# Gated DeltaNet stage of a two-layer decoder: a triangular solve merged to 128 ahead of the recurrence, squares and tanh written to PSUM banks, output norm once per group

## The chip, the cores and the metric

One core of a Trainium2 chip runs the whole program. The metric is the device time of one execution in microseconds (us). Engines are named as in the profile: PE (matmul; PEld its weight loads), DVE (VectorE), ACT (ScalarE), POOL (GpSimd) and SP (which here issues the DMAs). PSUM is the memory that PE writes its results to, in eight banks of 128 x 512 floats; the rest of the tiles lie in SBUF.

## The reference

A residual stream of 16 meta tokens and 256 tokens (272 x 2048, fp32) goes through two layers. The first mixes the tokens by a gated DeltaNet, the second by differential attention; each is followed by a squared-ReLU MLP of width 8192. The change lies in the first mixer:

```python
def gated_deltanet(h, w_in, conv_w, a_log, dt_bias, o_norm, w_out):
    proj = h @ w_in                        # 2048 -> q, k (16 heads), v, z (32 heads), beta and decay logits
    qkv = silu(causal_depthwise_conv(qkv, conv_w))         # 4 taps
    q, k = l2_normalize(q) * 128 ** -0.5, l2_normalize(k)
    beta, g = sigmoid(b_logit), -exp(a_log) * softplus(a_logit + dt_bias)
    o = chunk_gated_delta_rule(q, k, v, beta, g)
    o = rms_norm(o, o_norm) * silu(z)
    return o @ w_out

def step(S, (qc, kc, vc, bc, gc)):         # one chunk of tokens, S the state of a head
    G = cumsum(gc); decay = exp(G_i - G_j) for j <= i
    a_kk = strict_lower(bc * kc @ kc.T * decay)
    sol = triangular_solve(I + a_kk, [vc * bc, kc * bc * exp(G)])
    v_new = u - w @ S
    o = (qc * exp(G)) @ S + (qc @ kc.T * decay) @ v_new
    S = S * exp(g_last) + (kc * exp(g_last - G)).T @ v_new
```

## The kernel before

Activations lie with the features on the partitions. Each weight is read as 128 x 1024 floats twice per tile, and split: ACT copies it to a rounded `whi` (L137), DVE or POOL subtracts to get `wlo` (L141). A product is then three matmuls per 128 x 128 block, `whi*xh`, `wlo*xh` and `whi*xl` (L154, L157, L158), over 272 columns, in one PSUM bank out of a ring of four (`psm`).

The DeltaNet (`gdn`) goes over eight groups of four value heads and two key heads. A group takes 4 projections for its keys and queries (`keys`), 4 for its values (`values`) and 4 for its gates (`gates`). `conv_silu` runs the 4 taps (ACT L615, DVE L618), then tanh (ACT L620) and `out = (tanh + 1) * ac` on DVE (L621). `gate_out` multiplies the output of the group two places back by its slice of `w_out` and adds into `acc` (DVE L982).

The tokens of a group are cut in chunks of 128, 128 and 16. `products` makes for each chunk `ua`: in its first half the scaled, masked product of the keys (the triangle to solve, transposed and negated), in its second that of keys and queries. The 16 x 16 blocks on the diagonal go to DRAM, `solve` inverts all of them at once on DVE by rows (`forward`, L629 and L630), and they come back as `DT`, block-diagonal. POOL clears the blocks of `ua` on and below the 16-diagonal (`below`, L733).

`core` is the recurrence of the group. Its sub-generator `merge(c)` makes, from the 16-blocks, the inverses of the 32-blocks (`ps_e`, `ps_d`), has POOL clear `ua` below the 32-diagonal too, and multiplies them with it (`ps_n`, copied to `NT`). Then each of the chunks 0 and 1 takes the right-hand side `R`, applies `NT` three times in turn (`ps_a` L885, copies and adds L892, L896, L899), which sums the series over the four 32-blocks, and multiplies by the 32-block inverses: `ps_w` (L905), copied to `w`; DVE scales it to `ws` (L913). `ps_s` (from `ws`) gives the next state, `ps_o` (from `w`) the output. Chunk 2 needs no series. Each chunk ends in its output norm: four squares with row sums (ACT L942), eleven small DVE instructions (L944 to L948 with the seven of `rsqrt`, L105 to L111), one scaling (DVE L949); `turned` then transposes it (`ps_ot` L809) and multiplies it into the gates (L811).

The order of the instructions comes from `Flow`, a heap of generators: while projections are written, each k-step advances a clock by its nominal time, and a generator whose time has come writes its next piece between them. A generator that yields `step` (3.0, in the last group 2.0) asks to be called that much later. So the recurrence of group b-1 lies in small pieces between the projections of group b; after them the engines take their queues strictly in that order. In the last group there are only the products of `gate_out(6)` to lie between. `gate_out(7)` then ends the mixer: behind each of its 16 tiles DVE adds into `acc`, and `squares` adds up the squares of `acc` for the RMS norm (`add_ss`: ACT L183, for the last two tiles DVE L185; DVE adds into `ss` at L190). `token_means` sums `ss` over the partitions on PE (`pst`, L213), and the MLP waits for that.

## Time and profile before

| what | value |
|---|---|
| time, median of 3 runs | 3111.37 us (3111.28 to 3116.6) |
| time of the profiled execution | 3111.88 us |
| its span, first to last instruction | 3110.1 us |
| PE busy / PEld busy | 3010.9 us (97%) / 2946.4 us (95%) |
| DVE / ACT / POOL busy | 1930.1 us (62%) / 1443.3 us (46%) / 660.7 us (21%) |
| mean granted TensorE clock | 0.987 |
| the DeltaNet stage | from the start to about 1136 us |

The page gives for each engine the time in which it was busy, the span in 40 slices, and groups of instructions by line. "Idle before, releaser" is the time in which an engine stood still ahead of such an instruction, and what ended it. The view by windows gives busy times in chosen stretches of the span, with the mean clock that PE was granted. Times in us, unless marked ns. fp32 matmuls show as two records each (two passes); the split ones as one.

### The profile page before, as it was taken

To read this page: it belongs to the slowest core of one execution; us is meant where nothing else is said; L and a number is where in the kernel's file an instruction comes from. 1 tells how busy PE (TensorE), PEld (TensorE's weight loads), DVE (VectorE), ACT (ScalarE), POOL (GpSimd) and SP (SyncE) were. 2 spreads that over 40 slices of the span, in tenths; PEclk is the share of its full clock that TensorE was granted. 3 is DMA by queue.
4 is the path that set the end of the run, shared out by engine and by line. 5 is a ranking of instruction groups with operands and counts; after the bars stand their busy time and mean duration, and the time that the engine had idled before them with its cause. 6 is when DMAs were issued, how large, how long until landed. Compare 5 with 4: busy or idle time off the path is not lost. (4 is left out here: it accounts for less than half of the span.)

```text
span 3110.1 us, 57337 instructions
## 1 busy us (share of the span) xinstructions
PE 3010.9 (97%) x23779; PEld 2946.4 (95%) x23779; DVE 1930.1 (62%) x3449; ACT 1443.3 (46%) x2565; POOL 660.7 (21%) x398
## 2 busy tenths in 40 slices
PE   7999999999998889999999999999999999999998
PEld 6988999999998889999999999999999999999998
DVE  7676574766748485455555557777756555555555
ACT  4445454454544345434444334555555444444443
POOL 2544445545454351000000003400004000000000
PEclk9999999999999989999999999999999999999999
DMA  4433334334343335454444443443354555555553
GB/s 178 151 117 122 133 118 151 133 125 158 117 152 103 119 145 183 176 176 172 171 174 175 176 176 123 177 149 136 138 189 163 189 186 183 188 189 180 188 190 109
DMA packets 92468, 488.36 MB, mean 157 GB/s; under 512 B 29104, under 2 KB 32528, under 8 KB 34736
## 3 DMA queue, kind: packets, MB, share of 16 engines
q1 hardware_dynamic: 92208, 484.70, 43.7%
q8 instruction: 187, 3.06, 0.4%
q14 instruction: 73, 0.60, 0.1%
HBM read 481.41 MB, written 3.25 MB: 156 GB/s over the span
## 5 line engine op out<-in xcount | busy, mean ns | idle before, releaser
L137 ACT ACTIVATE whi<-wraw 128x1024 fp32r<-128x1024 f32 x890 | 939.2, 1058 | 1180.3 <-PE ps_dn L158 435.9
L141 DVE TENSOR_TENSOR wlo<-wraw,whi 128x1024 fp32r<-128x1024 f32 x682 | 841.4, 1237 | 717.1 <-ACT whi L137 715.9
L141 POOL TENSOR_TENSOR wlo<-wraw,whi 128x1024 fp32r<-128x1024 f32 x208 | 503.7, 2424 | 1584.3 <-ACT whi L137 1572.5
L158 PE MATMUL ps_dn<-yl,whi 128*128 128x272 f32 (+1 forms) x2048 | 584.5, 285 | 0.0
L157 PE MATMUL ps_dn<-yh,wlo 128*128 128x272 f32 (+1 forms) x2048 | 583.2, 285 | 0.0
L154 PE MATMUL ps_dn<-yh,whi 128*128 128x272 f32 (+1 forms) x2048 | 583.2, 285 | 0.0
L154 PE MATMUL ps_up<-xh,whi 128*128 128x272 f32 (+1 forms) x2048 | 582.9, 285 | 0.0
L158 PE MATMUL ps_up<-xl,whi 128*128 128x272 f32 (+1 forms) x2048 | 582.0, 285 | 0.1
L157 PE MATMUL ps_up<-xh,wlo 128*128 128x272 f32 (+1 forms) x2048 | 581.5, 285 | 0.2 <-DVE wlo L141 0.2
L154 PE MATMUL ps_in<-xh,whi 128*128 128x272 f32 x1520 | 463.4, 305 | 0.0
L157 PE MATMUL ps_in<-xh,wlo 128*128 128x272 f32 x1520 | 442.4, 291 | 16.7 <-DVE wlo L141 13.3
L158 PE MATMUL ps_in<-xl,whi 128*128 128x272 f32 x1520 | 444.0, 292 | 3.3 <-DVE xl L319 3.3
L154 PEld LDWEIGHTS ps_up<-xh,whi 128*128 128x128 f32 x2048 | 386.2, 189 | 0.5 <-ACT xh L402 0.2
L158 PEld LDWEIGHTS ps_dn<-yl,whi 128*128 128x128 f32 x2048 | 386.6, 189 | 0.0
L154 PEld LDWEIGHTS ps_dn<-yh,whi 128*128 128x128 f32 x2048 | 386.3, 189 | 0.0
L158 PEld LDWEIGHTS ps_up<-xl,whi 128*128 128x128 f32 x2048 | 385.6, 189 | 0.3 <-DVE xl L410 0.3
L157 PEld LDWEIGHTS ps_dn<-yh,wlo 128*128 128x128 f32 x2048 | 385.2, 188 | 0.0
L157 PEld LDWEIGHTS ps_up<-xh,wlo 128*128 128x128 f32 x2048 | 384.7, 188 | 0.5 <-DVE wlo L141 0.5
L157 PEld LDWEIGHTS ps_in<-xh,wlo 128*128 128x128 f32 x1520 | 290.2, 191 | 20.3 <-DVE wlo L141 14.9
L154 PEld LDWEIGHTS ps_in<-xh,whi 128*128 128x128 f32 x1520 | 289.7, 191 | 7.8 <-issue 5.1
L158 PEld LDWEIGHTS ps_in<-xl,whi 128*128 128x128 f32 x1520 | 289.5, 190 | 4.8 <-DVE xl L319 3.7
L399 POOL TENSOR_TENSOR hT<-hT,t_res 128x272 f32<-128x272 f32 (+1 forms) x40 | 34.9, 894 | 742.9 <-DVE t_res L391 698.2
(305 smaller groups left out, 4833.8 us busy)
## 6 DMA issues: line engine op xcount, KB each, us to landing
wraw<-w_up SPq DMA_DIRECT2D x128, 1024.0 KB
wraw<-w_down SPq DMA_DIRECT2D x128, 1024.0 KB
wraw<-w_in SPq DMA_DIRECT2D x97, 1024.0 KB
wraw<-w_out SPq DMA_DIRECT2D x32, 1024.0 KB
wraw<-w_kv SPq DMA_DIRECT2D x32, 1024.0 KB
wraw<-w_q SPq DMA_DIRECT2D x16, 1024.0 KB
wraw<-w_o SPq DMA_DIRECT2D x16, 1024.0 KB
gb<-g_dram SPq DMA_DIRECT2D x8, 544.0 KB
```

Source lines behind the costliest of these rows:

```text
L137: nc.scalar.activation(hi, part, AF.Copy)
L141: inst = eng.tensor_tensor(lo, part, hi.bitcast(F32), ALU.subtract)
L154: one = nc.tensor.matmul(ps, wh, rh, start=(k == 0), stop=False)
L157: nc.tensor.matmul(ps, wl, rh, start=False, stop=False)
L158: ring["mm"] = nc.tensor.matmul(ps, wh, rl, start=False, stop=(k == nk - 1))
L399: put(key, eng.tensor_tensor(h, h, ts[m][:, :N], ALU.add))
```

## The change

- **Solve.** `merge` now goes on from the 32-blocks to the 64-blocks and the whole 128-block, so that `dt` is the full inverse; the three applications of `NT` are gone, and `ps_w` multiplies `dt` with `R` at once. Each of three levels is a pair of products, of which only the blocks that change are made (64, 32 and 64 columns wide), with ACT copies between them, into the constant tiles `AE1`, `AE2`, `AE3`, `dt` and `dn`. Both calls of `below` are gone, as the products read only the blocks of `ua` that they need.
- **Banks.** `conv_silu` writes tanh over the projection's own PSUM bank; in the last `gate_out` the squares, but for the first and the last, go to the bank just added into `acc`; the output norm's squares go over `ps_o`.
- **Scaling by beta** (`ws`) is four ACT instructions from `ps_w`, ahead of the copy to `w`.
- **Output norm** once per group (12 columns) and for the last group still per chunk; the scaling is by ACT, four instructions per chunk. Each chunk's `turned` is added after that, 2.0 apart.
- One buffer fewer in the ring of work tiles (`G1`); `r0` shares the buffer of `ss`.

```diff
--- before.py
+++ after.py
-G1 = 8
+G1 = 7
...
+TGAP = 2.0
...
-    def add_ss(ss, src, m, N, eng):
+    def add_ss(ss, src, m, N, eng, bank=None):
 
         if m == 0:
             ss.append(npool.tile([P, L], F32, tag="ss", name="ss", bufs=1))
             return [nc.scalar.activation(ss[0][:, :N], src, AF.Square)]
-        sq = npool.tile([P, L], F32, tag="sq", name="sq", bufs=SQ)
-        if m < KT - NSQ or eng is nc.gpsimd:
+        if bank is None or m == KT - 1:
+            sq = npool.tile([P, L], F32, tag="sq", name="sq", bufs=SQ)
+        else:
+            sq = bank
+        if m < KT - NSQ or eng is nc.gpsimd or bank is not None:
             one = nc.scalar.activation(sq[:, :N], src, AF.Square)
         else:
             one = nc.vector.tensor_tensor(sq[:, :N], src, src, ALU.mult)
...
-    r0 = npool.tile([P, L], F32, name="r0", bufs=1)
+    r0 = npool.tile([P, L], F32, tag="ss", name="r0", bufs=1)
...
+    AE1 = gc.tile([P, HB, P], F32, name="AE1")
+    AE2 = gc.tile([P, HB, 64], F32, name="AE2")
+    AE3 = gc.tile([P, HB, 64], F32, name="AE3")
+    nc.gpsimd.tensor_copy(AE1, ident[:, None, :].broadcast_to([P, HB, P]))
+    nc.gpsimd.memset(AE2, 0.0)
+    nc.gpsimd.memset(AE3, 0.0)
 
     def conv_silu(ps, m, out):
 
         ac = gt.tile([P, L], F32, tag="g272", name="cv_a", bufs=GB)
-        th = gt.tile([P, L], F32, tag="g272", name="cv_x", bufs=GB)
         x = ps
         if m in unscaled:
-            x = th
+            x = gt.tile([P, L], F32, tag="g272", name="cv_x", bufs=GB)
             nc.vector.tensor_tensor(x, ps[:, :L], r0, ALU.mult)
         nc.scalar.activation(ac, x[:, :L], AF.Copy, scale=gdnc[:, m, 3:4])
         for j in (2, 1, 0):
             sh = 3 - j
             nc.vector.scalar_tensor_tensor(ac[:, sh:], x[:, :L - sh], gdnc[:, m, j:j + 1], ac[:, sh:],
                                            ALU.mult, ALU.add)
+        th = ps[:, :L]
         nc.scalar.activation(th, ac, AF.Tanh, scale=0.5)
         nc.vector.scalar_tensor_tensor(out, th, 1.0, ac, ALU.add, ALU.mult)
 
                 for bl in range(8):
                     q = slice(NM * bl, NM * bl + NM)
                     nc.sync.dma_start(scr[c, :, bl].rearrange("h j i -> j h i"), ua[q, :, 0, q])
-                below(ua, NM)
             else:
...
         step = STEP7[0] if b == NB - 1 else STEP
+        outs = []
+        ms = gt.tile([P, len(CH), HB], F32, tag="o_ms", name="o_ms")
+        nc.vector.memset(ms, 1.0)
         merged = {}
 
         def flat(t):
@@ -822,35 +828,68 @@
 
         def merge(c):
 
+            U = UA[c][:, :, 0, :]
+            X = DT[:, c].rearrange("p h (b i) -> p (h b) i", i=32)
             us = work("us")
             nc.gpsimd.affine_select(us.rearrange("p h (b i) -> p h b i", i=32),
-                                    UA[c][:, :, 0, :].rearrange("p h (b i) -> p h b i", i=32),
+                                    U.rearrange("p h (b i) -> p h b i", i=32),
                                     pattern=[[0, HB], [-32, 4], [0, 32]], base=0, channel_multiplier=1,
                                     compare_op=ALU.is_ge, fill=0.0)
-            below(UA[c], 32)
-            e16 = work("e16")
-            nc.vector.transpose(flat(e16), flat(DT[:, c]))
+            en = work("e16")
+            nc.vector.transpose(flat(en), flat(DT[:, c]))
             yield step
-            _, pE = bank("ps_e")
+
+            def small(name):
+                t = psc.tile([P, 512], F32, tag="c", name=name)
+                return t, t[:, 0:256].rearrange("p (h i) -> p h i", h=HB)
+
+            _, pE = small("ps_e")
+            ev = en.rearrange("p h (b i) -> p h b i", i=32)
             for hv in range(HB):
-                nc.tensor.matmul(pE[:, hv], us[:, hv], e16[:, hv], start=True, stop=True)
-            ae = work("ae")
-            nc.scalar.copy(ae, pE)
+                nc.tensor.matmul(pE[:, hv], us[:, hv], ev[:, hv, :, 0:NM], start=True, stop=True)
+            nc.scalar.copy(AE1.rearrange("p h (b i) -> p (h b) i", i=32)[:, :, 0:NM],
+                           pE.rearrange("p h (b i) -> p (h b) i", i=NM))
+            dt = work("d32")
+            dv = dt.rearrange("p h (b i) -> p (h b) i", i=32)
+            nc.scalar.copy(dv[:, :, 0:NM], X[:, :, 0:NM])
             yield step
-            _, pD = bank("ps_d")
+            _, pD = small("ps_d")
             for hv in range(HB):
-                nc.tensor.matmul(pD[:, hv], ae[:, hv], DT[:, c, hv], start=True, stop=True)
-            d32 = work("d32")
-            nc.vector.tensor_tensor(d32, DT[:, c], pD, ALU.add)
+                nc.tensor.matmul(pD[:, hv], AE1[:, hv], X[:, 4 * hv:4 * hv + 4, NM:32], start=True, stop=True)
+            nc.scalar.copy(dv[:, :, NM:32], pD.rearrange("p h (b i) -> p (h b) i", i=NM))
             dn = work("dn")
-            nc.vector.transpose(flat(dn), flat(d32))
+            nc.vector.transpose(flat(dn), flat(dt))
             yield step
-            _, pN = bank("ps_n")
+            pairs = lambda t, hv, k: t[:, hv].rearrange("p (b k i) -> p b k i", k=2, i=32)[:, :, k]
+            _, pE = small("ps_e")
             for hv in range(HB):
-                nc.tensor.matmul(pN[:, hv], dn[:, hv], UA[c][:, hv, 0, :], start=True, stop=True)
-            NT = work("NT")
-            nc.scalar.copy(NT, pN)
-            merged[c] = d32, NT
+                for k in range(2):
+                    nc.tensor.matmul(pE[:32, hv, 32 * k:32 * k + 32], U[:, hv, 64 * k + 32:64 * k + 64],
+                                     dn[:, hv, 64 * k:64 * k + 32], start=True, stop=True)
+            for k in range(2):
+                nc.scalar.copy(AE2[64 * k + 32:64 * k + 64, :, 32 * k:32 * k + 32], pE[:32, :, 32 * k:32 * k + 32])
+            yield step
+            pt, pD = small("ps_d")
+            pn = pt[:, 256:384].rearrange("p (h i) -> p h i", h=HB)
+            for hv in range(HB):
+                nc.tensor.matmul(pn[:32, hv], dt[:, hv, 32:64], AE2[:, hv, 0:32], start=True, stop=True)
+            for hv in range(HB):
+                nc.tensor.matmul(pD[:64, hv], AE2[:, hv], pairs(dt, hv, 1), start=True, stop=True)
+            nc.scalar.copy(dn[32:64, :, 0:32], pn[:32])
+            for k in range(2):
+                nc.scalar.copy(dt[64 * k:64 * k + 32, :, 64 * k + 32:64 * k + 64],
+                               pD[32 * k:32 * k + 32, :, 32 * k:32 * k + 32])
+            yield step
+            _, pE = small("ps_e")
+            for hv in range(HB):
+                nc.tensor.matmul(pE[:64, hv], U[:, hv, 64:128], dn[:, hv, 0:64], start=True, stop=True)
+            nc.scalar.copy(AE3[64:128], pE[:64])
+            yield step
+            _, pD = small("ps_d")
+            for hv in range(HB):
+                nc.tensor.matmul(pD[:64, hv], AE3[:, hv], dt[:, hv, 64:128], start=True, stop=True)
+            nc.scalar.copy(dt[:64, :, 64:128], pD[:64])
+            merged[c] = dt
             yield step
 
         yield from merge(0)
...
+                dt = merged[c]
+            else:
+                dt = DT3
+            if c > 0:
                 yield step
...
             _, pw = bank("ps_w")
             for hv in range(HB):
-                nc.tensor.matmul(pw[:n, hv], dt[:, hv, :], z[:n, hv], start=True, stop=True)
+                nc.tensor.matmul(pw[:n, hv], dt[:, hv, :], R[:n, hv], start=True, stop=True)
             if c == 2:
                 g["free"] = True
+            if c < 2:
+                ws = work("ws")
+                for hv in range(HB):
+                    nc.scalar.activation(ws[:, hv], pw[:, hv], AF.Copy, scale=sup[:, c, hv // 2, hv % 2:hv % 2 + 1])
             w = work("w")
             nc.scalar.copy(w[:n], pw[:n])
-            if c < 2:
-                ws = work("ws")
-                sb = sup[:, c].rearrange("p h r -> p (h r)")[:, :, None].broadcast_to([P, HB, P])
-                nc.vector.tensor_tensor(ws, w, sb, ALU.mult)
             yield step
             if c < 2:
                 pS2, pS2v = bank("ps_s2")
@@ -936,19 +957,26 @@
                     nc.vector.scalar_tensor_tensor(ov[:n, hv], ov[:n, hv], eG[:n, c, HB * b + hv:HB * b + hv + 1],
                                                    po[:n, hv], ALU.mult, ALU.subtract)
 
-            o2 = work("o2")
-            ms = gt.tile([P, HB], F32, tag="o_ms", name="o_ms")
             for hv in range(HB):
...
+                nc.scalar.activation(po[:n, hv], ov[:n, hv], AF.Square, accum_out=ms[:n, c, hv:hv + 1])
+            outs.append((c, o, n, ov))
+            if b == NB - 1 or c == len(CH) - 1:
+                c0 = outs[0][0]
+                k = HB * len(outs)
+                pn = n if len(outs) == 1 else P
+                mc = ms[:pn, c0:c + 1].rearrange("p c h -> p (c h)")
+                rqc = rq[:pn, c0:c + 1].rearrange("p c h r -> p (c h r)")
+                nc.vector.tensor_tensor(mc, mc, rqc, ALU.mult)
+                nc.vector.tensor_tensor(mc, mc, rqc, ALU.mult)
+                nc.vector.tensor_scalar(mc, mc, 1.0 / P, EPS, ALU.mult, ALU.add)
+                ri = rsqrt(mc, "rso%d" % k, [P, k], pn)
+                nc.vector.tensor_tensor(ri, ri, rqc, ALU.mult)
+                for i, (cc, oo, nn, ot) in enumerate(outs):
+                    for hv in range(HB):
+                        nc.scalar.activation(ot[:nn, hv], ot[:nn, hv], AF.Copy, scale=ri[:nn, HB * i + hv:HB * i + hv + 1])
+                    flow.add(turned(cc, oo, nn, ot), STEP7[1] if b == NB - 1 else OTURN + TGAP * i)
+                outs = []
             g["chunk"] = c + 1
-            flow.add(turned(c, o, n, ov), STEP7[1] if b == NB - 1 else OTURN)
             yield step
 
     def halves(g):
@@ -981,9 +1009,10 @@
                     else:
                         added = nc.vector.tensor_tensor(acc[:, m, :], acc[:, m, :], ps[:, :L], ALU.add)
                     if b == NB - 1 and m > 0:
-                        squares(m - 1, L, ssm, acc, 1, added)
+                        squares(m - 1, L, ssm, acc, 1, added, spent)
                         if m == KT - 1:
-                            squares(m, L, ssm, acc, 1)
+                            squares(m, L, ssm, acc, 1, None, ps)
+                spent = ps
         if b + 1 < NB:
             flow.add(halves(gs[b + 1]))
```

How the order moves, at three places. First PE at the end of the last group's recurrence, where the last products of `gate_out(6)` lie between its pieces. Before, the last rows up to the first product of `gate_out(7)` (`ps_ks`, `ps_qs`: state times keys and queries for chunk 2):

```order
L157 MATMUL ps_out<-oh,wlo 128x272
L158 MATMUL ps_out<-ol,whi 128x272
L866 MATMUL ps_ks<-S,kq 16x256 x2
L870 MATMUL ps_qs<-S,kq 16x256 x2
L905 MATMUL ps_w<-R,DT_261 16x128 x4
L809 MATMUL ps_ot<-ident,ov 128x128 x4
L930 MATMUL ps_o<-w,UA_11074 16x128 x4
L809 MATMUL ps_ot<-ident,ov 128x16 x4
L154 MATMUL ps_out<-oh,whi 128x272
```

With the change:

```order
L158 MATMUL ps_out<-oh,wlo 128x272
L159 MATMUL ps_out<-ol,whi 128x272
L926 MATMUL ps_w<-R,d_12075 128x128 x4
L939 MATMUL ps_s_12287<-ws,kn 128x256 x2
L951 MATMUL ps_o<-w,UA 128x128 x4
L905 MATMUL ps_ks<-S,kq 16x256 x2
L909 MATMUL ps_qs<-S,kq 16x256 x2
L926 MATMUL ps_w<-R,DT_261 16x128 x4
L812 MATMUL ps_ot<-ident,ov 128x128
L951 MATMUL ps_o<-w,UA_10975 16x128
```

Chunk 1's `ps_w`, `ps_s` and `ps_o`, which had 18 and 12 products of `gate_out(6)` behind them, now stand behind the last of these products.

Second, DVE at the end of `gate_out(7)`. Before (`ss` is the running sum, `sq` a square in SBUF):

```order
L982 TENSOR_TENSOR acc<-acc,ps_out 128x272
L190 TENSOR_TENSOR ss<-ss,sq 128x272
L185 TENSOR_TENSOR sq<-acc 128x272
L105 TENSOR_SCALAR rs_y<-pst 128x3
L106 SCALAR_TENSOR_TENSOR rs_t<-rs_y 128x3
```

With the change (`ps_out` as the second operand of L194 is the bank that holds the square):

```order
L1010 TENSOR_TENSOR acc<-acc,ps_out 128x272
L194 TENSOR_TENSOR ss<-ss,ps_out 128x272
L106 TENSOR_SCALAR rs_y<-pst 128x3
L107 SCALAR_TENSOR_TENSOR rs_t<-rs_y 128x3
L108 TENSOR_TENSOR rs_t<-rs_t,pst 128x3
```

The adds stand where they stood, with another operand; the last squares have left DVE.

Third, ACT at the end of a merge and the scaling behind it, with the change, in the second group (`d` is `dt`):

```order
L878 COPY dn<-ps_d 32x4x32
L880 COPY d_3220<-ps_d 32x4x32 x2
L886 COPY AE_264<-ps_e 64x256
L891 COPY d_3220<-ps_d 64x4x64
L932 ACTIVATE ws<-ps_w,sc_sup 128x128 x2
L138 ACTIVATE whi<-wraw 128x1024
L932 ACTIVATE ws<-ps_w,sc_sup 128x128 x2
L934 COPY w<-ps_w 128x512
```

Before, one copy stood here:

```order
L615 ACTIVATE cv_a<-ps_in,gdnc 128x272
L709 ACTIVATE dec<-gb,ngG 16x16 x3
L137 ACTIVATE whi<-wraw 128x1024
L620 ACTIVATE cv_x<-cv_a 128x272
L709 ACTIVATE dec<-gb,ngG 16x16
L909 COPY w<-ps_w 128x512
```

So ACT has the steps of the merge and the scaling in its queue, with the conversions of the weights between them.

36 lines of the change are left out of this document (2 added, 34 removed).

## The prediction

> **What bounds the kernel now.** I read the busy times first, then PE by stages, then what ended its waits, then the rows around the two longest. By stages of the program, from the view by windows (columns: window, length, busy time and instructions of PE, PEld, DVE, ACT and POOL, granted clock, DMA share, GB/s):
>
> ```profile
> 40.00:360.00 320.00, 294.10 (x2192) 280.69 (x2193) 223.24 (x483) 155.75 (x377) 149.00 (x85) 0.96 0.37 128
> 360.00:1074.00 714.00, 690.24 (x5373) 665.79 (x5372) 449.40 (x1021) 343.36 (x765) 351.28 (x179) 1.00 0.38 133
> 1074.00:1089.00 15.00, 7.07 (x36) 3.60 (x36) 9.75 (x39) 5.04 (x20) 0.00 (x0) 0.71 0.21 72
> 1089.00:1136.00 47.00, 35.86 (x239) 34.85 (x238) 34.57 (x48) 17.13 (x28) 25.49 (x10) 0.80 0.51 184
> 1136.00:1900.00 764.00, 764.00 (x6059) 763.48 (x6058) 426.78 (x531) 331.94 (x439) 23.76 (x25) 1.00 0.48 172
> ```
>
> PE bounds it. Behind 1136 us it never stops up to 1900, and the change touches nothing from there on. In the DeltaNet stage it is busy nearly always too, so two things are worth time: work taken from PE, and its idle time, 320.00 - 294.10 = 25.9, 23.8, 7.9 and 11.1 us by row. The clock adds to the last two stages (0.71 and 0.80). The waits of PE from 40 to 1074 us, with total, times and longest:
>
> ```profile
> PE ps_in L157 <- DVE wlo L141: 12.8, 6, 5.2
> PE ps_s L918 <- DVE ws L913: 9.8, 7, 3.4
> PE ps_u L705 <- DVE UA L711: 6.8, 5, 1.4
> PE ps_out L154 <- DVE acc L982: 4.4, 4, 2.5
> PE ps_g L579 <- issue: 3.5, 1, 3.5
> PE ps_in L157 <- POOL wlo L141: 3.4, 4, 1.6
> ```
>
> The rest of the 49.7 us, 9.0, are smaller waits, and nearly all wait for DVE, which is 63 to 70% busy there. Why DVE is late shows in the durations of one shape (min/median/max ns; the sum of squares by its own lines):
>
> ```profile
> L621 DVE SCALAR_TENSOR_TENSOR vt<-cv_x,cv_a x32: 402/443/2484, 78.7 to 981.5; 128x272 f32<-128x272 f32 x32
> L791 DVE SCALAR_TENSOR_TENSOR oT<-zt,ps_in x32: 414/426/439, 107.5 to 1037.0; 128x272 f32<-128x272 f32 x32
> L190 DVE TENSOR_TENSOR ss<-ss,sq x14: 429/2133/2434, 1096.3 to 1126.7; 128x272 f32<-128x272 f32 x14
> ```
>
> With both tensors in SBUF the same work takes 0.4 or 2.4 us; with one of them in PSUM it never exceeds 0.44. 2.4 us is what POOL needs for one `wlo` (mean 2424 ns, first row of the next fence). So a DVE instruction with two SBUF operands stands still behind a POOL instruction; one that reads a bank does not.
>
> **The change part by part.**
>
> *DVE.* Grouped rows of the stage, for what leaves it or gets a bank:
>
> ```profile
> L141 POOL TENSOR_TENSOR wlo<-wraw,whi 128x1024 fp32r<-128x1024 f32 x196 | 475.0, 2426 | 534.8 <-ACT whi L137 523.1 <-DMA scr<-UA 9.0 <-issue 1.9
> L621 DVE SCALAR_TENSOR_TENSOR kq<-cv_x,cv_a 128x272 f32<-128x272 f32 x32 | 35.6, 1113 | 20.5 <-ACT cv_x L620 20.5
> L949 DVE TENSOR_TENSOR ov<-ov,rs_y 128x512 f32<-128x512 f32 (+1 forms) x24 | 24.6, 1025 | 0.3
> L913 DVE TENSOR_TENSOR ws<-w,sc_sup 128x512 f32<-128x512 f32 x16 | 14.8, 926 | 3.7 <-ACT w L909 3.7
> L899 DVE TENSOR_TENSOR z<-z,ps_a 128x512 f32<-128x512 f32 x16 | 10.9, 683 | 6.7 <-PE ps_a L885 6.7
> L105 DVE TENSOR_SCALAR rs_y<-o_ms 128x4 int32<-128x4 int32 (+1 forms) x24 | 14.6, 608 | 0.3
> L733 POOL TENSOR_SCALAR_AFFINE_SELECT UA<-UA 128x512 f32<-128x512 f32 x32 | 29.2, 916 | 20.4 <-DMA scr<-UA 19.5
> ```
>
> Tanh through the bank: 64 instructions from about 1.1 to 0.43 us, 43 us. L949 and L913 go, 39 us; so do the adds of the three applications and of the merge, three times the size of L899's row, 33 us. The norm runs 10 times instead of 24: of its eleven small instructions L105 alone takes 608 ns on the mean, and at 0.3 us for one the 14 runs are 46 us. Together some 160 us of the 673 that DVE is busy from 40 to 1074. POOL loses the 29 us of L733 and its wait for DMAs.
>
> Of the waits I take `wlo` from 12.8 to 6, `ws` (now from ACT) from 9.8 to 4, UA from 6.8 to 4, acc from 4.4 to 2, POOL's from 3.4 to 2, the small ones from about 9 to 5, and leave L579's: some 24 us off. What ACT gets instead: per chunk four scalings, some ten copies of blocks, and four scalings of the output. With
>
> ```profile
> L772 ACT ACTIVATE nv<-ps_v,sc_nk x96: 342/343/370, 85.8 to 986.2; 128x128 f32<-128x128 f32 x64, 16x128 f32<-16x128 f32 x32
> L838 ACT COPY ae<-ps_e x16: 568/585/589, 142.6 to 1042.4; 128x512 f32<-128x512 f32 x16
> ```
>
> 8 x 0.34 us, plus ten copies at 0.3 (the smaller the block, the nearer to the smallest row), less three copies of 0.58, is about 4 us a chunk, some 65 us in all, on an engine that is 48% busy from 40 to 1074 (499 of 1034 us). It lies beside PE's projections; the cover is the fill between two pieces, mostly 18 to 27 products of 0.126 us (764 us for the 6059 of the last row by stages). Where the order leaves less, PE waits: in the second group most rungs of the merge have 3 to 8 products between them, and in each group `ps_w` and `ps_s` of chunk 1 stand some five apart, so four scalings (1.4 us) are not covered. I charge 4 us for that. The squares over `ps_o` hold a bank of the recurrence some 2 us longer, and tanh over a projection's bank holds that until L621; of that ring four projections of 6 us each are the cover, and nothing is charged. Stalls: -20 us. Two of the longest also cost clock:
>
> ```profile
> 204.00:214.00 10.00, 6.59 (x31) 6.04 (x29) 9.81 (x21) 1.38 (x2) 2.34 (x1) 0.66 0.17 55
> 336.00:347.00 11.00, 6.41 (x33) 5.91 (x32) 5.99 (x10) 1.34 (x2) 3.75 (x4) 0.69 0.10 19
> ```
>
> The first holds the 3.4 us for `ws`, the second one for `wlo`. Each loses 0.34 x 10 us, less what falls in the idle time: 5 us for both, if the waits shrink as taken.
>
> *PE's work.* Per chunk 24 fp32 matmuls (three products of the merge, three applications, four heads each) become 32: 8 with 128 columns of weights, 12 with 32, 12 with 64. Rows of a timeline (start, duration):
>
> ```profile
> 141.41 1.06 PE L836 MATMUL ps_e<-e,us 128*128 128x128 f32 x8
> 142.22 0.37 PE L154 MATMUL ps_in<-xh,whi 128*128 128x272 f32 x1
> 142.44 0.28 PE L157 MATMUL ps_in<-xh,wlo 128*128 128x272 f32 x1
> ...
> 86.70 0.23 PE L705 MATMUL ps_u<-kq 128*16 128x32 f32 x2
> 86.86 0.39 PE L158 MATMUL ps_in<-xl,whi 128*128 128x272 f32 x1
> ```
>
> Eight passes with 128 columns of weights put off the next product but one to 1.03 us behind the first of them, of which one product is 0.126: 0.90 us, 0.113 each with the change-over. Two passes with 16 columns of weights take at most 0.16, 0.08 each. Weight loads give the lower end:
>
> ```profile
> L905 PEld LDWEIGHTS ps_w<-z,d x128: 186/192/192, 170.3 to 1068.5; 128*128 128x128 f32 x128
> L905 PEld LDWEIGHTS ps_w<-R,DT x64: 87/92/92, 221.6 to 1077.8; 16*16 16x16 f32 x64
> ```
>
> 100 ns for 112 columns, so a pass with 32 columns would be 0.086 us shorter and one with 64 0.057: 0.027 and 0.056, mean 0.042. The new products have 48 narrow passes and 16 full ones. At 0.06 (between 0.042 and 0.08): 16 x 0.113 + 48 x 0.06 = 4.7 us for the 48 x 0.113 = 5.4 of before; 0.7 less in each of 16 chunks, -12 us. The ends: at 0.042 -26 us, at 0.113 (no gain from narrowness) +29.
> The Trainium skill (TensorE: Matmul & The Clock Gate, section LDWEIGHTS) makes a load its columns divided by 1.2 ns, whatever the rows: 27 ns for 32, 53 for 64, 107 for 128. As an estimate by that page alone a chunk would go from 5.1 to 3.6 us, -24 us in all; the slope of the two rows above agrees with it.
>
> *The end of the last group.* Before, the last products of `gate_out(6)` end, and the rest of the recurrence stands alone:
>
> ```profile
> 1067.80 1.05 PE L905 MATMUL ps_w<-z,d 128*128 128x128 f32 x8
> ...
> 1074.30 1.04 PE L866 MATMUL ps_ks<-S,kq 128*16 128x256 f32 x4
> ...
> 1080.07 0.81 PE L809 MATMUL ps_ot<-ident,ov 128*128 128x128 f32 x4 [1.87 <-DVE ov L949]
> ...
> 1087.25 0.58 PE L809 MATMUL ps_ot<-ident,ov 16*128 16x16 f32 x4 [4.55 <-DVE ov L949]
> ```
>
> With the change two merges of six rungs instead of three make the ladder longer than three applications made it, so chunk 1's `ps_w`, `ps_s` and `ps_o` lose their fill. From `ps_w` to `ps_ks` took 6.5 us with 30 products (3.8 us) in it. Alone it takes 0.9 for `ps_w`, 1.4 for the scalings, 0.9 for `ps_s`, 1.1 for the state and some 0.2 of passing on at each, 5 us. The fill is done earlier, so 5 - (6.5 - 3.8) = 2.3 us are new, and the half clock (0.71 in this stage) lasts a little longer: +3 us, 0 to +6.
>
> *The norm behind `gate_out(7)`.*
>
> ```profile
> 1116.32 0.28 PE L206 MATMUL pst<-eps,ident 128*128 128x3 f32 x2
> 1127.18 1.15 PE L213 MATMUL pst<-inv,ss 128*16 128x1 f32 x6 [10.57 <-DVE ss L190]
> ```
>
> DVE needs 0.42 us for `acc` and 2.1 for `ss` per tile, where PE takes 12 products, 1.5 us. At 0.43 for `ss` DVE keeps up: the last `acc` and `ss` end 1 us behind PE's last product, so `pst` starts near 1117.4, 9.8 us earlier. Without the gap the clock need not fall for the 7 us that follow; I add 2 us and take one off for the last square, which waits on ACT behind a conversion: -11 us, -8 to -13.
>
> *Sum:* -20 - 5 - 12 + 3 - 11 = -45. 3110.1 - 45 = 3065 us of span; the profiled execution took 1.8 us more than its span and 0.5 more than the median of its runs: 3067 us.
>
> **The rivals.**
> - *The waits are only handed on* (22%). DVE is freed, but PE then waits as long for ACT's copies, or for the rungs of the merge. For it: each new rung is matmul, ACT copy, matmul, and ACT's queue holds conversions of 1.06 us. Against it: 18 to 27 products between most rungs, 2 to 3 us. Stalls and their clock give nothing: -12 + 3 - 11 = -20, 3091 us.
> - *A bank does not free DVE* (4%): reading `ac` or `ss` from SBUF is enough to wait for POOL. Against it the row of L791, which reads `zt` from SBUF too. The norm keeps its 11, half of the stalls stay: 3090 us.
> - *Narrow passes cost as much as full ones* (7%): +29 instead of -12, 3108 us. Against it the 16-column row.
> - *Slower: the ladder itself* (5%). Six rungs for each of two chunks in eight groups are 96 waits, if ACT's copy (0.3 to 0.6 us) and a conversion ahead of it (1.06) come out uncovered each time. At 0.8 us a rung that is 77 us, 3144 us. It decides from 0.5 us a rung on, where less than a dozen products lie between; the order has that in the second group and, for want of fill, at the end.
>
> **How the numbers follow.** My forecast has 62%. Its own range is 3040 to 3088: work -26 to 0, stalls with clock -34 to -12, chain and norm as bounded. Handed-on waits lie just above it, so the range for 8 in 10 is 3036 to 3098. A difference under 0.2% (6 us) can't be told from no change. Faster by more: the forecast and the first two rivals (0.88) and a part of the third (0.02), 0.90; the same, the rest of the third and the mild end of the ladder, 0.06; slower, the rest of the ladder, 0.04.
>
> **What would show it.** L621 and the adds into `ss` at 0.43 us with no 2.4 us among them; no wait for `ws` over 2 us and clock 1.00 near 205 and 340; PE's wait before `pst` under 2 us; the passes with 32 and 64 columns under 0.08 us apart; the gap at the end of the last group some 2 us longer. PE waiting for L850 to L891's copies in the middle groups, or ACT ending most of PE's waits, would make it wrong; so would PE's summed idle time from 40 to 1074 us above 40.

## The result, and the profile after

The changed kernel takes 3093.84 us (median of 4 runs, 3091.89 to 3095.47), the kernel before 3111.55 us beside it: a ratio of 0.9941, 95% interval 0.9926 to 0.9957, 18 us faster. The forecast was 3067. Its direction was right and its range held the time, but the gain is less than half of what was forecast, and part of it comes from a place that the forecast did not name. The profiled execution has a span of 3090.2 us, 19.9 less than before. By stages, in the view by windows (columns as in the prediction):

```profile
40.00:360.00 320.00, 298.66 (x2296) 280.02 (x2295) 188.03 (x422) 173.66 (x450) 140.86 (x79) 0.96 0.37 130
360.00:1074.00 714.00, 690.15 (x5542) 651.74 (x5541) 369.20 (x858) 387.72 (x961) 322.33 (x156) 1.00 0.38 134
1074.00:1089.00 15.00, 7.69 (x36) 4.58 (x35) 6.81 (x32) 6.59 (x22) 0.00 (x0) 0.63 0.00 1
1089.00:1136.00 47.00, 44.95 (x325) 44.05 (x325) 28.44 (x66) 23.76 (x40) 31.00 (x18) 0.90 0.50 184
```

DVE is busy 557 us instead of 673 from 40 to 1074 us. PE's idle time there is 21.3 + 23.9 = 45.2 us; it was 49.7. The waits of PE in that stretch (total, times, longest):

```profile
PE ps_in L158 <- DVE wlo L142: 8.6, 5, 5.2
PE ps_in L158 <- POOL wlo L142: 7.8, 9, 1.7
PE ps_u L715 <- DVE UA L721: 7.0, 5, 1.4
PE ps_g L583 <- DVE ba_nat L575: 5.3, 1, 5.3
...
PE ps_in L155 <- ACT whi L138: 1.5, 4, 0.4
...
PE ps_s L939 <- ACT ws L932: 1.0, 2, 0.8
PE ps_w L926 <- ACT d L891: 0.8, 1, 0.8
PE ps_out L155 <- DVE acc L1010: 0.7, 1, 0.7
```

What the banks were to do to single instructions, they do. By form (count, then busy time and mean ns of one, then idle time before them):

```profile
L631 DVE SCALAR_TENSOR_TENSOR vt<-ps_in,cv_a 128x272 f32<-128x272 f32 x32 | 13.8, 430 | 16.7 <-ACT ps_in L630 16.6 <-PE ps_v L773 0.2
L194 DVE TENSOR_TENSOR ss<-ss,ps_out 128x272 f32<-128x272 f32 x14 | 6.0, 432 | 1.5 <-ACT ps_out L187 1.5
```

The longest of these instructions takes 0.44 us now; the 2.4 us of before are gone. So the wait ahead of `pst` shrank from 10.57 us to 2.05:

```profile
1115.54 1.15 PE L217 MATMUL pst<-inv,ss 128*16 128x1 f32 x6 [2.05 <-DVE ss L194]
```

Where the 19.9 us came from, by the starts of the same matmuls in both traces (us; the first MLP and the whole by their ends):

| landmark | before | after | difference |
|---|---|---|---|
| first `ps_u` of the fourth group | 420.9 | 415.2 | -5.7 |
| first `ps_u` of the last group | 942.0 | 940.4 | -1.6 |
| first product of `gate_out(6)` | 1034.5 | 1029.8 | -4.7 |
| first product of `gate_out(7)` | 1088.7 | 1086.9 | -1.8 |
| end of the products of the first MLP | 1913.7 | 1902.3 | -11.4 |
| end | 3110.1 | 3090.2 | -19.9 |

So the DeltaNet up to its last `gate_out` gave 1.8 us where 34 were forecast; the norm gave 9.6; and 8.5 came behind 1900 us, where none of the edits seemed to reach. And the four steady groups in the middle, 420.9 to 942.0 before and 415.2 to 940.4 after, became longer, from 130.3 to 131.3 us each on the mean.

### The profile page after: what moved, and what is told of

It is laid out like the page before. It is cut to its first block, busy times and chain, and to the rows that moved or that the text cites. A ratio compares the mean times of both kernels' runs of the same rounds, so it can differ in the third digit from the quotient of the medians.

```text
span 3090.2 us, 57790 instructions
## 1 busy us (share of the span) xinstructions
PE 3005.3 (97%) x24035; PEld 2922.1 (95%) x24035; DVE 1792.1 (58%) x3213; ACT 1507.5 (49%) x2839; POOL 622.1 (20%) x369
## 5 line engine op out<-in xcount | busy, mean ns | idle before, releaser
L142 POOL TENSOR_TENSOR wlo<-wraw,whi 128x1024 fp32r<-128x1024 f32 x208 | 496.6, 2392 | 1651.5 <-ACT whi L138 1627.3
```

The costliest lines, as they stand in the source:

```text
L142: inst = eng.tensor_tensor(lo, part, hi.bitcast(F32), ALU.subtract)
```

## The experiments

At first the theory was: the narrow rungs (pieces of the merge with 32 or 64 columns of weights) pay for a change-over, time that PE loses where narrow passes and full ones meet, so the solve gives PE nothing; and ACT, which now has the scalings, stands in its queue where DVE stood before. The rival was the forecast's own sum, with one part of the change giving its gain back. Ratios below are to the kernel before, run beside each; the whole change is 0.9941. "Group" is the distance between the first `ps_u` of two steady groups.

### The parts by themselves

The kernel before, with the two bank edits alone:

```diff
+        th = ps[:, :L]
...
-                        squares(m - 1, L, ssm, acc, 1, added)
+                        squares(m - 1, L, ssm, acc, 1, added, spent)
```

> The kernel before with the two bank edits alone: tanh over the projection's bank, and the squares of the last gate_out through the bank just spent. Theory: the norm behind the last gate_out gives 10 us (PE's wait ahead of pst from 10.6 to about 2, and less half clock), and the stalls in the DeltaNet give 3 to 6 more: 3095 to 3099, most of the whole change's gain. Rival (the gain is spread over the parts as forecast): the norm's 11 and about half of the stalls' 25, some 12: 3087 to 3091.

Measured: 0.9946 (0.9933 to 0.9958), 3096.97 us, as the theory had it. The two bank edits alone give nearly as much as the whole change. In the trace 10.9 us of the 14.5 lie between the first product of `gate_out(7)` and the end of the first MLP: they are the norm's.

The kernel before, with the change's `merge` and without the three applications and `below`. This run also has the seven work buffers and `r0` in the buffer of `ss`; its expectation does not name the latter, and it turned out to matter:

```diff
+                dt = merged[c]
...
-                p1 = apply(R)
```

> The kernel before with the new solve alone (six rungs per chunk, no below, seven buffers); tanh, squares, beta and norm as before. Theory: the solve alone gains no PE time, steady groups of 129.9 us become 130 to 131, and the last group's end is 2 to 5 us longer: 3110 to 3120, no gain over 3111.5. Rival (the forecast's work term): 12 us less of PE work and 2 to 4 us less of stalls, 3095 to 3100.

Measured: 0.9978 (0.9969 to 0.9987), 3107.6 us. Its row for one group beside that of the kernel before (first fence: before; second: the solve alone):

```profile
420.90:550.70 129.80, 126.14 (x986) 121.58 (x985) 84.35 (x194) 63.50 (x143) 65.98 (x35) 1.00 0.39 137
```

```profile
683.30:813.60 130.30, 126.24 (x1018) 119.97 (x1017) 80.44 (x188) 65.91 (x157) 61.00 (x31) 1.00 0.39 136
```

PE is busy 126.1 us a group with the old solve and 126.2 with the new one; the forecast had 1.4 less. In its trace `gate_out(7)` begins 3.1 us later than in the kernel before, and the last MLP takes 5.4 us less. So the 6.5 us that it is faster lie mostly in the last MLP, and come with `r0`, as the run with that line alone shows below.

The other way round, the changed kernel with that part undone:

```diff
-                dt = merged[c]
+                dt, NT = merged[c]
...
+                p1 = apply(R)
```

> The changed kernel with the solve put back: merge to 32, three applications, both calls of below, eight buffers in the ring. Banks, scalings by ACT and the norm per group stay. Theory (each narrow rung pays a change-over of some 0.3 us, so that the new solve costs PE as much as the old one): from the trace of the changed kernel a chunk's six rungs take 5.4 us of PE, the same as the six of before; with 30 instead of 35 separate stretches per steady group the group gets 0.5 to 1 us shorter, so the time is 0 to 8 us under the 3094 of the changed kernel, 3086 to 3094. Rival (the narrow passes do save the 12 us of the forecast and something else gave them back): 12 us and what DVE's adds cost come on top, 3103 to 3112.

Measured: 0.995 (0.9938 to 0.9963), 3098.4 us, not to be told from the changed kernel by these intervals; the group takes 132.5 us, PE is busy in it for 126.8 as in the changed kernel, and a new wait of 1.8 us for `vt` came in. Neither expectation holds: the old solve costs PE no more and no less than the new one, but moving its pieces moves the waits.

The changed kernel without its scalings by ACT and its norm per group:

```diff
-                    nc.scalar.activation(ws[:, hv], pw[:, hv], AF.Copy, scale=sup[:, c, hv // 2, hv % 2:hv % 2 + 1])
+                nc.vector.tensor_tensor(ws, w, sb, ALU.mult)
...
-            outs.append((c, o, n, ov))
+            nc.vector.tensor_tensor(ov[:n], ov[:n], ri[:n, :, None].broadcast_to([n, HB, P]), ALU.mult)
```

> The changed kernel with two parts undone: ws again one multiplication on DVE from w, and the output norm again once per chunk, scaled by DVE. Banks and the new solve stay. Theory (the norm per group and the scalings by ACT cost what the rest gained: ACT stands still for DVE ahead of its conversions): banks alone took 17 us off and the new solve alone 6.5; together 21 to 24, ratio to before 0.9923 to 0.9933, steady groups of 129.3 to 129.8 us instead of 131.2. Rival (the parts that relieve DVE overlap and saturate at the same point): no better than the changed kernel, ratio 0.9941, steady groups near 131.

Measured: 0.9945 (0.9933 to 0.9958), groups of 129.8 to 130.5 us. The rival was right: the solve on top of the banks gives nothing. The groups are shorter than with the norm per group, but the early part is longer (the fourth group starts at 421.7 us instead of 415.2), so the two parts undone neither cost nor bring anything in the sum that these runs can tell.

The gain behind 1900 us pointed at a line that looked idle, `r0` in the buffer of `ss`. Rows of the same 600 us of the last MLP, the kernel before and the changed one:

```profile
2400.00:3000.00 600.00, 600.00 (x5073) 600.00 (x5073) 339.49 (x411) 270.67 (x350) 0.55 (x1) 1.00 0.53 188
```

```profile
2400.00:3000.00 600.00, 600.00 (x5114) 600.00 (x5114) 338.82 (x412) 268.96 (x342) 0.00 (x0) 1.00 0.52 187
```

PE never stops in either, at full clock, on the same products (128x256 there); yet on the mean one starts every 118.3 ns before and every 117.3 after.

That line alone, in the kernel before:

```diff
-    r0 = npool.tile([P, L], F32, name="r0", bufs=1)
+    r0 = npool.tile([P, L], F32, tag="ss", name="r0", bufs=1)
```

> The kernel before with one line of the change alone: r0 shares the buffer of ss, which only moves what is laid out behind it in SBUF by 1088 bytes. Theory (the layout sets the pitch of the last MLP's products: 739.6 us from its first matmul to its last in the kernels with r0 apart, 733.7 to 734.3 in all those with r0 shared): -6 us, all of it behind 2350 us, the DeltaNet stage unchanged to 0.5 us; ratio 0.9975 to 0.9985. Rival (the pitch comes with another part, the seven buffers or the new tiles): no change, ratio 1.000.

Measured: 0.9989 (0.998 to 0.9997), 3108.4 us, and in its trace

```profile
2400.00:3000.00 600.00, 600.00 (x5114) 600.00 (x5113) 341.73 (x414) 273.64 (x355) 4.02 (x4) 1.00 0.52 189
```

One line that only shifts tiles in SBUF gives the faster pitch; in the traces the last MLP takes 734.3 us from its first matmul to its last instead of 739.6. The measured 3.7 us are a little under that. The first MLP, over 272 columns, keeps its pitch: 6059 products from 1136 to 1900 us before, 6057 after. Which tile's new address does it, and why, is open. So is where the rest of the 8.5 us comes from; some 2.3 of them lie between the two MLPs.

And both, the bank edits and this line, in the kernel before:

> The kernel before with tanh and the squares through banks, and r0 in the buffer of ss: nothing of the new solve, of beta by ACT and of the norm per group. Theory (the banks' 17 us and the layout's 6 add up, as they lie in different stages): ratio 0.992 to 0.9935, 3089 to 3093, as good as the whole change or better. Rival (the layout needs the other parts): 0.9946 as with the banks alone.

Measured: 0.9929 (0.9917 to 0.9941), 3091.4 us: the banks and this line are as good as the whole change, and no worse than the run above that has the new solve on top of them (0.9945). Everything else in the change, the new solve, beta by ACT and the norm per group, sums to nothing that these runs can tell.

### What a narrow rung costs

Four rungs of the changed kernel with the products around them, from its timeline: full width; 64 columns of weights; 32 and then 64 columns, with two passes of `ps_u` behind them; and sixteen passes with 32 columns:

```profile
412.32 0.29 PE L159 MATMUL ps_in<-xl,whi 128*128 128x272 f32 x1
412.45 1.00 PE L858 MATMUL ps_d<-DT,AE 128*128 128x64 f32 x8
413.25 0.37 PE L155 MATMUL ps_in<-xh,whi 128*128 128x272 f32 x1
413.47 0.28 PE L158 MATMUL ps_in<-xh,wlo 128*128 128x272 f32 x1
...
429.26 0.29 PE L159 MATMUL ps_in<-xl,whi 128*128 128x272 f32 x1
429.48 0.68 PE L885 MATMUL ps_e<-dn,UA 128*64 128x64 f32 x8
430.09 0.39 PE L155 MATMUL ps_in<-xh,whi 128*128 128x272 f32 x1
430.31 0.29 PE L158 MATMUL ps_in<-xh,wlo 128*128 128x272 f32 x1
...
424.54 0.29 PE L159 MATMUL ps_in<-xl,whi 128*128 128x272 f32 x1
424.76 0.44 PE L875 MATMUL ps_d<-AE,d 128*32 128x32 f32 x8
425.13 0.68 PE L877 MATMUL ps_d<-d,AE 128*64 128x64 f32 x8
425.74 0.23 PE L715 MATMUL ps_u<-kq 128*16 128x32 f32 x2
425.90 0.40 PE L155 MATMUL ps_in<-xh,whi 128*128 128x272 f32 x1
426.14 0.29 PE L158 MATMUL ps_in<-xh,wlo 128*128 128x272 f32 x1
...
417.81 0.29 PE L159 MATMUL ps_in<-xl,whi 128*128 128x272 f32 x1
418.03 0.69 PE L867 MATMUL ps_e<-dn,UA 128*32 128x32 f32 x16
418.65 0.39 PE L155 MATMUL ps_in<-xh,whi 128*128 128x272 f32 x1
418.88 0.29 PE L158 MATMUL ps_in<-xh,wlo 128*128 128x272 f32 x1
```

From product to second product the full rung takes 1.15 us, the one with 64 columns 1.05: of that, 0.25 are two products, so 0.90 and 0.80; in the same way the other two take 1.19 (less 0.16 for `ps_u`) and 0.82. By the starts of the single passes in the trace the full ones are 0.112 apart, those with 64 columns 0.058 and with 32 columns 0.031, so narrower is cheaper, and more so than the forecast took. But the first narrow pass starts 0.22 us behind the last product, where a full one starts 0.13 behind it, and the next product comes 0.15 behind the last narrow pass, where it comes 0.08 behind a full one. Beside their eight passes (0.90 and 0.46 us) the full rung costs nothing, the narrow one 0.34. It saves 0.1 us, not 0.4.

> The changed kernel with the narrow rungs of 16, 8 and 8 passes each written in two halves of two heads, 0.6 of the order's clock apart: the same passes, in about 25 more separate stretches (not every split finds products to lie between). Theory of the change-over: each further stretch costs 0.3 us, steady groups of 131.2 become 132.0 to 133, in all +6 to +11 us, 3100 to 3105. Rival (a narrow pass costs 0.075 us wherever it stands): no change, 3092 to 3096.

```diff
             for hv in range(HB):
+                if hv == 2:
+                    yield SPLIT
                 nc.tensor.matmul(pE[:64, hv], U[:, hv, 64:128], dn[:, hv, 0:64], start=True, stop=True)
```

Measured: 0.9972 (0.9962 to 0.9982), 9.7 us over the changed kernel by the ratios. PE is busy 128.3 us a group instead of 126.8. One of the split rungs:

```profile
523.08 0.29 PE L160 MATMUL ps_in<-xl,whi 128*128 128x272 f32 x1
523.29 0.45 PE L890 MATMUL ps_e<-dn,UA 128*64 128x64 f32 x4
523.67 0.40 PE L156 MATMUL ps_in<-xh,whi 128*128 128x272 f32 x1
523.90 0.29 PE L159 MATMUL ps_in<-xh,wlo 128*128 128x272 f32 x1
```

Half the passes take 0.59 from product to product, not half of 0.83: the change-over is paid a second time. For PE's work the theory is borne out. It does not make the whole 9.7 us, though: in the trace the first product of `gate_out(6)` comes 5.7 us later than in the changed kernel, and from there to `gate_out(7)` it takes 63.0 us instead of 57.1, where the last split rungs stand alone and PE waits 1.2 and 0.5 us for copies between them.

The other way round, with fewer stretches:

> The changed kernel with the second chunk's merge two rungs behind the first one's instead of after it, written in the same pieces: the same passes in four stretches fewer per group, and chunk 1's block is ready earlier in the last group. Theory of the change-over (0.3 us where two narrow rungs meet, about half where a narrow one meets a full one): 0.7 to 1.2 us a group, 5 to 10 us in all, and up to 3 more at the end of the last group: ratio 0.990 to 0.9925. Rival (cost per pass): no change in the groups, at most the end's 3 us, ratio 0.993 to 0.994.

```diff
-        yield from merge(0)
-        flow.add(merge(1), step)
+        m0, m1 = merge(0), merge(1)
+        for k in range(7):
+            next(m0)
+            if k >= 2:
+                next(m1)
+            yield step
+        flow.add(m1, step)
```

Measured: 0.9957 (0.9943 to 0.9971), where both expectations had the changed kernel's time or less: no gain, and by the overlapping intervals not surely a loss. Fewer change-overs were paid for with waits: four of 4.6 to 8.2 us in the steady groups, for a `wlo` on DVE and for `vt`. Its last group, though, went well (see below).

### ACT's queue

In the steady group of the changed kernel a conversion is late: ACT stands 3.86 us for DVE ahead of the squares of the third chunk, then works off what has piled up, and the `wlo` behind it comes late on POOL, and PE waits for that (ACT, POOL, PE):

```profile
458.66 0.27 ACT L961 ACTIVATE ps_o<-ov 16x128 f32<-16x128 f32 x1 [3.86 <-DVE ov L957]
...
460.88 1.04 ACT L138 ACTIVATE whi<-wraw 128x1024 fp32r<-128x1024 f32 x1
```

```profile
462.00 2.36 POOL L142 TENSOR_TENSOR wlo<-wraw,whi 128x1024 fp32r<-128x1024 f32 x1 [4.59 <-ACT whi L138]
```

```profile
464.41 0.39 PE L158 MATMUL ps_in<-xh,wlo 128*128 128x272 f32 x1 [1.23 <-POOL wlo L142]
```

Four edits of the changed kernel's order (the last one on the kernel with the banks and `r0`): the output's scalings 6 to 10 of the order's clock later; the scalings back on DVE; the squares of the third chunk later (`if c == 2 and b < NB - 1: yield 4.0` ahead of them); `UGAP` 2.4 instead of 1.2.

> The changed kernel with the twelve scalings of the output per group taken out of the piece that ends the norm: they are written 6, 8 and 10 of the order's clock later, four each, so that ACT's queue does not stand behind DVE's norm; transposing comes at the same times as before. Theory: PE's waits for wlo and whi near the end of a steady group (1.7, 0.9 and 0.4 us) fall to about the 1.6 us of the kernel with the banks alone, groups of 129.8 to 130.4 instead of 131.2, in all -5 to -11 us, ratio 0.9906 to 0.9925. Rival (ACT's stand behind the squares of the last chunk or its sheer load makes these waits): within 3 us of the changed kernel, ratio 0.993 to 0.995.

Measured: 0.9934 (0.9922 to 0.9947); the waits of a group are the same to 0.1 us. That theory falls: the scalings delay nothing.

> The changed kernel with the output's scaling on DVE again, one instruction per chunk, but still with one norm per group. Theory: ACT does not wait for the norm any more, DVE gets three instructions of about 0.7 to 2.4 us back, which queue ahead of a wlo: groups of 130 to 131 us, -2 to -8 us, ratio 0.9915 to 0.9935. Rival: scaling is not the cause, no change, ratio 0.9941.

Measured: 0.9966 (0.9954 to 0.9979), slower. On DVE the scalings stand ahead of a `wlo`: PE waits 2.6 us for it in each group, which takes 133 us. ACT was the better place.

> The changed kernel with the squares of a group's third chunk, and with them the norm, written 4 of the order's clock later, but for the last group. Theory (ACT stands 3.9 us ahead of these squares for DVE, and a conversion behind them is late, which gives PE's waits of 1.2 and 0.4 + 0.9 us a group): groups of 129.3 to 130.3 instead of 131.2, in all -5 to -12 us, ratio 0.990 to 0.9925. Rival (the conversions are late for want of a buffer or by POOL, and ACT's stand is covered): groups of 131, ratio 0.993 to 0.995.

Measured: 0.9931 (0.9917 to 0.9944), 3090.1 us. The groups are 129.8 us, as expected, but the waits for `whi` and `wlo` became one of 2.3 us for POOL's `wlo`, and the time is only some 3 us less than that of the changed kernel, which is within the intervals.

> The kernel with the banks and r0 shared, and in addition the pieces of the keys' products 2.4 instead of 1.2 of the order's clock apart, as a try at the best version: PE's wait of 1.4 us a group for UA (DVE behind POOL) gets cover. If it goes without a new wait: -8 to -11 us against the same kernel with 1.2, ratio 0.989 to 0.990. If the later end of the pieces moves the wait to the next product: no change.

Measured: 1.0017 (1.0008 to 1.0026), 27 us over the kernel without that edit. The wait for `UA` went, and one of 4.8 to 6.3 us for a `wlo` on DVE came in each group. In this try, as with the joined merges, moving pieces about in the order only moved the waits.

### The end of the last group

> The changed kernel, in the last group alone with the second chunk's merge two rungs behind the first one's and in the same pieces; the other groups as they are. Theory (the ladder at the end is what is left over: from the first product of gate_out(6) to the first of gate_out(7) the changed kernel needs 57 us and the kernel before 54, where the kernel with all groups joined, slower before that, needed 36.5 with nearly the whole recurrence between the products): 38 to 47 us there, -10 to -18 in all, ratio 0.988 to 0.991. Rival (the recurrence just takes its place among the gates' projections, and PE does the same work earlier): -2 to -4 us, ratio 0.9925 to 0.994.

```diff
+        m1 = merge(1)
+        for k, _ in enumerate(merge(0)):
+            if b == NB - 1 and k >= 2:
+                next(m1)
+            yield step
+        flow.add(m1, step)
```

Measured: 0.9917 (0.9902 to 0.9931), 3087.7 us. From `gate_out(6)` to `gate_out(7)` it takes 50.4 us instead of 57.1, where the theory had 38 to 47; the ratio lies between the theory's range and the rival's. The theory was drawn too far: the kernel with all groups joined needs 43.5 us there by its trace (1048.5 to 1092.0), not the 36.5 of the expectation. `ps_w`, `ps_s` and `ps_ks` have found cover; the last norm and its transposing have not:

```profile
1076.98 1.16 PE L812 MATMUL ps_ot<-ident,ov 16*128 16x16 f32 x4 [4.72 <-ACT ov L980]
```

> The changed kernel with both: the third chunk's squares 4 of the order's clock later, and the last group's merges joined. If they add up: ratio 0.987 to 0.990, 3072 to 3082, under both kernels. If the end's gain is only moved: 0.992 to 0.993.

Measured: 0.99 (0.9883 to 0.9916), 3082.7 us: the two add up, within the noise of such small gains.

### POOL

A chain that comes back in each steady group is this (DVE, then POOL, then PE, in the changed kernel):

```profile
418.22 2.32 DVE L110 SCALAR_TENSOR_TENSOR rs_t<-rs_t 128x12 f32<-128x12 f32 x1
...
420.54 0.47 DVE L721 SCALAR_TENSOR_TENSOR UA<-ps_u,sc_nc,dec 128x256 f32<-128x256 f32 x1
```

```profile
418.14 2.37 POOL L142 TENSOR_TENSOR wlo<-wraw,whi 128x1024 fp32r<-128x1024 f32 x1 [2.31 <-ACT whi L138]
```

```profile
421.07 0.70 PE L715 MATMUL ps_u<-kq 128*128 128x256 f32 x2 [1.40 <-DVE UA L721]
```

A DVE instruction over twelve columns, with two operands in SBUF, starts just behind a subtraction on POOL and lasts as long as that; `UA` stands behind it, and PE behind `UA`. The banks took this from three kinds of instructions. Others on DVE still have it, and POOL's share of the work was untouched. The Trainium skill (SBUF — State Buffer, section Who interferes with whom) says that a DVE instruction with two SBUF inputs contends with a GpSimd instruction that reads SBUF, and calls the lock on the ports that the two share exclusive; the rows agree, 2.32 us behind 2.37.

Some instructions even got more of it. The products of `forward` in the solve by rows (tile `fw_t`, two operands in SBUF) are the same 120 before and after the change; the view by windows for their line alone gives, after the length of the stretch, their busy time (before, then after):

```profile
40.00:1074.00 1034.00, 74.58 (x120) 0.99 0.38 132
```

```profile
40.00:1074.00 1034.00, 93.67 (x120) 0.99 0.38 133
```

So 19 us of what DVE was relieved of came back as time behind POOL. With half and with a quarter of the subtractions on POOL, in the runs that follow, these 120 take 79.1 and 69.5 us.

> The changed kernel with half of the subtractions wlo on POOL in the DeltaNet instead of three quarters, the others on DVE, which the change left 54% busy from 40 to 1074 us. Theory (the stalls that stayed are made by POOL: DVE's instructions with two SBUF operands stand behind its 2.4 us subtractions, and POOL's own wlo come late): POOL's busy time from 463 to about 320 us, DVE's from 557 to about 640, PE's idle time from 45 to 30 to 38 us, ratio 0.989 to 0.992. Rival (what DVE was relieved of was not what PE waited for, and DVE's order decides): the same or worse, ratio 0.994 to 0.998.

```diff
-PQ = 2
+PQ = 1000
```

Measured: 0.9883 (0.9869 to 0.9898), 3076.9 us, 17 us under the changed kernel and more than expected, with PE's idle time at 37.2 us, as expected. The fourth group starts at 397.7 us instead of 415.2; the steady groups stay at 131.2.

> The kernel before, with half instead of three quarters of the subtractions wlo on POOL in the DeltaNet, and nothing else. Theory (the change makes room on DVE, and only that room lets DVE take them over): DVE, 65% busy from 40 to 1074 us, goes above 72%, PE's idle time changes by less than 5 us, ratio 0.996 to 1.002. Rival (POOL makes the stalls whatever DVE's load, and the room was not needed): as with the changed kernel some 17 us off, nearly all before 420 us, ratio 0.993 to 0.9955.

Measured: 0.9995 (0.9986 to 1.0004), no change. Rows from 40 to 1074 us: the kernel before, the same with half on POOL, and the changed kernel with half on POOL:

```profile
40.00:1074.00 1034.00, 984.34 (x7563) 946.47 (x7564) 672.64 (x1504) 499.11 (x1141) 500.28 (x263) 0.99 0.38 132
```

```profile
40.00:1074.00 1034.00, 988.43 (x7568) 949.45 (x7567) 726.67 (x1561) 499.18 (x1137) 361.00 (x203) 0.98 0.38 132
```

```profile
40.00:1074.00 1034.00, 996.77 (x7881) 939.06 (x7882) 614.22 (x1373) 567.43 (x1434) 318.88 (x173) 0.98 0.39 134
```

In the kernel before DVE is then 70% busy, and PE waits 1.6 us a group for a `wlo` on DVE where it waited 0.8. In the changed kernel it is 59% busy, and PE gains. So the change made something that half on POOL can use. That it is the room on DVE is read from these busy shares and this wait; no run changes DVE's load alone.

> The changed kernel with all three: half of the wlo on POOL, the third chunk's squares later, the last group's merges joined. The steady group with half on POOL waits 1.5 us for a conversion on ACT that stands behind those squares. Theory (they add up, as they lie in the early groups, the steady ones and the end): steady groups of 129 to 130 instead of 131.3, 8 us less at the end, ratio 0.9835 to 0.986, 3060 to 3070. Rival (one takes the other's place): 0.987 to 0.989.

Measured: 0.9856 (0.9842 to 0.9869), 3069.8 us; groups of 130.1 us. The three gains add up nearly (24 us under the changed kernel; 17 and 11 by themselves).

> The kernel with all three, but a quarter of the wlo on POOL instead of half. If POOL's subtractions are still what DVE stands behind: POOL's busy time falls to some 180 us from 40 to 1074, and 3 to 8 us come off against the kernel with half, ratio 0.981 to 0.984. If DVE is by then what is late: slower than with half, with PE's waits for DVE's wlo above 1.5 us, ratio 0.987 or more.

```diff
-                on_pool = ring.get("pool") and (q == 1 or ring["n"] // 2 % PQ == 1)
+                on_pool = ring.get("pool") and q == 1 and ring["n"] // 2 % 2 == 1
```

Measured: 0.9754 (0.9741 to 0.9767), 3036.3 us, 58 us under the changed kernel and 77 under the kernel before: the version that beats both. The last step alone gives 33 us, where 3 to 8 were expected. Its stage and one of its groups:

```profile
40.00:1074.00 1034.00, 1018.78 (x8127) 965.32 (x8126) 665.16 (x1485) 585.18 (x1464) 196.45 (x123) 0.99 0.41 140
...
391.20:516.90 125.70, 125.70 (x1019) 119.69 (x1018) 80.38 (x178) 70.94 (x177) 22.24 (x14) 1.00 0.41 141
```

PE does not stop once in a steady group, and the twelve-column instruction of above is back at its own length (changed kernel, then this one, 40 to 1074 us):

```profile
L110 DVE SCALAR_TENSOR_TENSOR rs_t<-rs_t 128x12 f32<-128x12 f32 x15 | 17.4, 1163 | 0.1
```

```profile
L111 DVE SCALAR_TENSOR_TENSOR rs_t<-rs_t 128x12 f32<-128x12 f32 x15 | 2.5, 166 | 0.1
```

DVE, with three times as many subtractions (186 instead of 62), is busy 665 us: less than in the kernel before, though the stretch holds more of the program here. Over the same work, from the first `ps_kn` to the first product of `gate_out(7)`, PE is idle for 49.8 us in the changed kernel, 32.2 with all three edits and half on POOL, and 11.5 here. So it was POOL's share that held most of the waits that the change left. What a quarter on POOL does to the kernel before, or to the banks alone, was not run.

## Why the prediction was right and where it was wrong

- **Reading of the bound: right.** PE bounds the stage, and DVE is late because it stands behind POOL: the banks' rows (0.43 us) and the last run show both.
- **Stalls, -20: failed; -4.5 came.** The step that failed is the one from DVE's relief, taken as 160 us, to waits that shrink by half. Two things in it were wrong. The instructions that left DVE or got a bank gave about the 160 us in sum of their durations, but `fw_t` took 19 us more behind POOL, and small instructions had overlapped with others, so that DVE's busy time fell by 115 us. And a wait is not a share of DVE's load. `ws` (9.8 to 1.0) and `acc` (4.4 to 0.7) went further than forecast, as they lost their DVE instruction or DVE its stand; but `wlo` on DVE fell from 12.8 to 8.6, not 6, `UA` stayed (6.8, now 7.0), POOL's `wlo` rose from 3.4 to 7.8 instead of falling to 2, PE's wait ahead of `ps_g` rose from 3.5 to 5.3, and the smaller ones from 9.0 to 14.8 instead of falling to 5. The chains that were followed here, to `UA` and to POOL's `wlo`, have a POOL subtraction in them, and the change left three quarters of the subtractions on POOL.
- **Clock, -5: the two named spells went, others came.** Near 205 and 340 us the granted clock is 1.00 now. The row for 40 to 360 us has 0.96 as before: the spell of lower clock near 120 us is longer (0.71 from 120 to 130 us, where it was 0.94), and there is a new one near 245 (0.83 from 240 to 250), both behind waits.
- **PE's work, -12: nothing came.** This term was mis-sized. The narrow passes cost no more than was taken (0.058 and 0.031 us, against 0.06), but the sum left out the change-over of 0.34 us at the ends of a narrow stretch; the row that priced full passes could not show it, as a full stretch has none. A chunk's rungs are 2 x 0.90 + 0.82 + 1.19 + 2 x 0.80 = 5.4 us by the rows above, against 5.4 before and 4.7 forecast.
- **End of the last group, +3: right in size.** From `gate_out(6)` to `gate_out(7)` 54.1 became 57.1 us. Up to `ps_ks` 1.7 us are new, where 2.3 were forecast; the rest lies behind it.
- **Norm, -11: right.** 9.6 us came, with 2.05 us left ahead of `pst`, where under 2 was said.
- **Not foreseen: -8.5 behind 1900 us**, of which the layout makes 5 to 6. The forecast said that the change touches nothing there; it had passed over the line on `r0`. That the measured time lies inside the range is luck to this extent: without these 8.5 us it would be near 3102, outside it.
- **The rivals.** "Handed on" named a time, 3091, that is near the measured one, by another sum: its -12 did not come and the layout's did. Its mechanism is half of it. ACT ends few of PE's waits directly (7.5 us of 45), but its stand ahead of the squares makes a `wlo` on POOL late, for which PE waits 1.2 us (the rows of ACT's queue). Most waits were not handed to ACT, they stayed with DVE and POOL. "A bank does not free DVE" is refuted by the rows of 0.43 us, and "the ladder itself" by the waits: of the rungs' copies PE waited for one, 0.8 us (`ps_w` for `d`). "Narrow passes cost as much" is refuted too: at 0.113 us each a chunk's 64 passes would take 7.2 us, and they take 5.4. What narrow stretches do cost is their ends.
- The mark set for being wrong, more than 40 us of idle time from 40 to 1074, was reached with 45.2.

## What to carry to other kernels

Freed time on an engine that does not bound is worth little by itself: ask which chain ends each wait, and move the work that stands in it. Price a small matmul rung among other products by the distance from product to second product, not by its passes. And after a change of tiles, compare the stages that it did not touch.
